# A decoder block on one core: the moving operand of every fp32r matmul is read from its last column to its first, and the accumulator is written in the same order

## The chip, the cores and the metric

The kernel runs on one core of a Trainium2 chip. The metric is the device time of one execution in microseconds (us); smaller is better. The profile calls the engines PE (TensorE, the matrix engine), PEld (its weight loads), DVE (VectorE), ACT (ScalarE), POOL (GpSimd) and SP (SyncE, whose queue carries most DMA transfers). SBUF is the on-chip memory from which PE reads, PSUM the one into which it writes and accumulates.

## What is computed

One decoder block for 256 tokens of width 2048, in float32. Cut to its matrix products:

```python
x = x + 0.5 * swiglu(rmsnorm(x, ffn1_norm), ffn1_w_gate, ffn1_w_up, ffn1_w_down)
proj = rmsnorm(x, mix_norm) @ w_in                      # 2048 x 11264
dq, dk, dv, hq, hf, hi, hg, gate_a, gate_b = split(proj)
y_a = diff_attention(dq, dk, dv, ...)                   # 8 heads
y_b = hgrn2(hq, hf, hi, hg, ...)                        # gated linear recurrence
merged = sigmoid(gate_a) * (y_a @ w_branch_a) + sigmoid(gate_b) * (y_b @ w_branch_b)
x = x + merged @ w_out
x = x + 0.5 * swiglu(rmsnorm(x, ffn2_norm), ffn2_w_gate, ffn2_w_up, ffn2_w_down)
ple = rmsnorm(p @ w_ple_proj, ple_post_norm)
x = x + sigmoid(rmsnorm(x, ple_gate_norm) @ w_ple_gate) * ple
```

The feed-forward width is 5632. In the changed kernel every output has the same value at the same place as before.

## The kernel before

**The products.** All the large products go through one function, `group` (lines 141 to 150). The weights come in blocks of 256 rows by 512 columns, stored as a tile of 128 partitions x 2 x 512. There are 804 such blocks, in the order of the list `plan` (lines 73 to 95): the gate and up matrices of the first feed-forward net, its down matrix, the input projection, the two branch matrices, the output matrix, the second feed-forward net, and the two matrices of the embedding.

**fp32r and three terms.** A float32 operand is split in two fp32r tiles: a high part and the rest. `wh` and `wl` are the two parts of a weight block; `AH` and `AL` (or `hH`/`hL`, `mH`/`mL`, `yaH`/`yaL`, `ybH`/`ybL`, `pH`/`pL`) those of the activations. A product is the sum of three matmuls: high by high (line 148), high by low weights (line 149), low by high weights (line 150).

**Which operand moves.** The stationary operand, loaded into PE's array ahead of each matmul, is a 128 x 128 piece of the activations (128 rows of the sum by 128 tokens). The moving operand, which streams through the array, is half a weight block: 128 partitions by 512 columns, one column after the other. The output is an accumulator `acc` in PSUM of 128 tokens by 512 columns, float32. A block serves two halves of its rows (`k2`) and two token tiles (`tt`), so `group` issues 2 x 2 x 3 = 12 matmuls. In the last product alone, the second token tile is computed as two column halves, in tiles `ms` of 256 columns (`last_product`).

**Order of the work.** The order on every engine is written out by hand. `stream` walks through the blocks of a product: it calls `prep` for the block three places ahead (a DMA on SP's queue into `raw`, line 112; a copy on ACT that makes `wh`, line 114; a subtraction on DVE that makes `wl`, line 115), issues the 12 matmuls, and then lets the smaller tasks go on by a step. These tasks hold the rest of the block: transposes on PE through PSUM tiles `tp` (lines 209, 219, 362), attention (lines 440 to 478), the recurrence (lines 589 to 641), norms and gates on ACT and DVE. Four buffers `acc` take turns, two to a product, so a product writes into the buffers of the product before the last one. `raw` has five buffers, `wh` and `wl` four.

The functions that the change touches, and what calls them:

Of the kernel before, what the change touches and what calls it, by code (L numbers as in the profile page):

```python
# [48 lines left out]
def block_kernel(ctx: ExitStack, tc: tile.TileContext, a: dict, out: bass.AP):  # L49
    nc = tc.nc  # L50
# [15 lines left out]
    def tcol(tt):  # L66
        return slice(tt * P, (tt + 1) * P)
# [73 lines left out]
    def group(n, act, last, dsts):  # L141
        AH, AL = act
        wh, wl = ready[n]
        for k2 in range(2):
            kt = 2 * plan[n][2] + k2
            for dst, tt, cols in dsts:
                hi, lo = AH[:, kt, tcol(tt)], AL[:, kt, tcol(tt)]
                nc.tensor.matmul(dst, hi, wh[:, k2, cols], start=(kt == 0), stop=False)  # L148
                nc.tensor.matmul(dst, hi, wl[:, k2, cols], start=False, stop=False)  # L149
                nc.tensor.matmul(dst, lo, wh[:, k2, cols], start=False, stop=(kt == last))  # L150

    def stream(w, c, groups, act, dsts, held=0):
        for g in range(groups - held):
            n = at[0]
            assert plan[n] == (w, c, g), (plan[n], w, c, g)
            if owed[0]:
                advance()
            prep(n + AHEAD)
            group(n, act, 2 * groups - 1, dsts)
            at[0] += 1  # L160
            owed[0] = True
            if g < groups - 1:
                advance()
# [6 lines left out]
    def last_product(w, c, groups, act):  # L170
        dsts = [(T(psA, [P, NB], "acc"), 0, WHOLE)]
        for cols in (slice(0, HALF), slice(HALF, NB)):
            dsts.append((T(psM, [P, NB], "ms")[:, :HALF], 1, cols))
        stream(w, c, groups, act, dsts, AHEAD)
        for d in dsts:
            for i in range(AHEAD):
                group(at[0] + i, act, 2 * groups - 1, [d])
            yield d
# [717 lines left out]
```

## Time and profile before

| | |
|---|---|
| time before, median of 3 runs | 2307.64 us (2307.3 to 2307.93) |
| the profiled execution's own time | 2307.12 us |
| its span, first to last instruction | 2304.2 us |
| granted TensorE clock, mean | 1.000 |
| PE busy | 2296.5 us, 10564 instructions |
| DVE busy | 1270.9 us, 1381 instructions |
| ACT busy | 1041.0 us, 1270 instructions |
| moved by DMA | 432.55 MB, mean 188 GB/s |

The busy time of an engine is the time in which at least one of its instructions is open. On PE a matmul's record goes on while the next one has begun, so the records of PE sum to more than its busy time; the distance from one start to the next is what a matmul costs in a dense stream. The median of the three runs is 0.52 us above the profiled execution, which is 2.92 us above its own span. A line of the profile names the line of the program, the engine, the operation, output and inputs, the shape, and how often it ran (x).

### The profile page before, as it was taken

How to read it: one execution, taken by the hardware profiler on the slowest of the kernel's cores; microseconds unless marked ns; L12 is line 12 of the kernel's file. 1: busy time of each engine (PE TensorE's matmuls, PEld its weight loads, DVE VectorE, ACT ScalarE, POOL GpSimd, SP SyncE). 2: the span in 40 equal slices, each digit the busy share in tenths (PEclk: the TensorE clock that was granted, in tenths of full speed). 3: DMA queues.
4: the chain of work that ended last, by engine and by line, in shares of the span. 5: the costliest groups of instructions: out<-in, count | busy, mean ns of one | idle time of the engine just before them, and what ended most of it. 6: DMA issues, size and time to landing. Idle time of an engine off the chain costs nothing.

```text
span 2304.2 us, 27206 instructions
## 1 busy us (share of the span) xinstructions
PE 2296.5 (100%) x10564; PEld 1903.1 (83%) x10564; DVE 1270.9 (55%) x1381; ACT 1041.0 (45%) x1270; POOL 39.4 (2%) x38
## 2 busy tenths in 40 slices
PE   9999999999999999999999999999999999999999
PEld 7888888888888888888888888888888888888887
DVE  5555555544444576667765555545555555444456
ACT  6444444444444455553334444544444444344454
POOL 0000000000000100000000000000000000000000
PEclk9999999999999999999999999999999999999999
DMA  8666666666666655554555666666666656666664
GB/s 295 192 190 192 187 189 191 185 192 190 190 186 196 204 159 168 186 173 154 160 159 181 186 189 184 184 192 191 191 186 190 192 186 191 192 190 191 192 211 150
DMA packets 120464, 432.55 MB, mean 188 GB/s; under 512 B 13773, under 2 KB 14181, under 8 KB 120208
## 3 DMA queue, kind: packets, MB, share of 16 engines
q1 hardware_dynamic: 118800, 426.33, 59.7%
q0 software_dynamic: 1248, 4.43, 0.5%
q8 instruction: 82, 1.34, 0.2%
q14 instruction: 46, 0.38, 0.0%
q10 hardware_dynamic: 288, 0.07, 0.0%
HBM read 428.67 MB, written 2.11 MB: 187 GB/s over the span
## 4 chain that ended last, share of the span: by engine, by line
PE 98%; DMA 1%; DVE 0%; ACT 0%; SPq 0%; issue 0%; ACTq 0%
PE acc L148 31%; PE acc L150 31%; PE acc L149 31%; PE tp L209 1%; PE ms L616 1%; DMA raw<-in_gu 1%; PE tp L219 0%; PE ms L440 0%; PE ms L149 0%; PE ms L150 0%; PE ms L148 0%; PE ms L589 0%; PE tp L362 0%; ACT wh L114 0%; PE tp L477 0%
## 5 line engine op out<-in xcount | busy, mean ns | idle before, releaser
L115 DVE TENSOR_TENSOR wl<-raw,wh 128x1024 fp32r<-128x1024 f32 (+1 forms) x805 | 984.1, 1224 | 877.8 <-ACT wh L114 875.6
L114 ACT CAST wh<-raw 128x1024 fp32r<-128x1024 f32 (+1 forms) x805 | 843.8, 1049 | 932.3 <-PE acc L150 904.6
L148 PE MATMUL acc<-wh,AH 128*128 128x512 f32 x2224 | 878.8, 395 | 0.7 <-ACT wh L114 0.5
L150 PE MATMUL acc<-wh,AL 128*128 128x512 f32 x2224 | 868.4, 390 | 0.0
L149 PE MATMUL acc<-wl,AH 128*128 128x512 f32 x2224 | 866.9, 390 | 1.2 <-DVE wl L115 1.0
L150 PEld LDWEIGHTS acc<-wh,AL 128*128 128x128 f32 x2224 | 417.6, 188 | 88.5
L149 PEld LDWEIGHTS acc<-wl,AH 128*128 128x128 f32 x2224 | 418.4, 188 | 85.9 <-DVE wl L115 2.8
L148 PEld LDWEIGHTS acc<-wh,AH 128*128 128x128 f32 x2224 | 418.0, 188 | 85.1 <-ACT wh L114 1.6
L148 PE MATMUL acc<-wh,hH 128*128 128x512 f32 x704 | 275.6, 392 | 0.0
L150 PE MATMUL acc<-wh,hL 128*128 128x512 f32 x704 | 274.5, 390 | 0.0
L149 PE MATMUL acc<-wl,hH 128*128 128x512 f32 x704 | 274.2, 390 | 0.0
L149 PEld LDWEIGHTS acc<-wl,hH 128*128 128x128 f32 x704 | 132.3, 188 | 27.3
L150 PEld LDWEIGHTS acc<-wh,hL 128*128 128x128 f32 x704 | 132.2, 188 | 27.4
L148 PEld LDWEIGHTS acc<-wh,hH 128*128 128x128 f32 x704 | 132.2, 188 | 27.0
L263 ACT ACTIVATE s<-acc,rowr 128x256 f32<-128x256 f32 x86 | 40.6, 475 | 48.9 <-PE acc L150 48.9
L183 ACT CAST hH<-tp 128x512 fp32r<-128x512 f32 x44 | 25.8, 587 | 73.9 <-PE tp L209 73.9
L184 DVE TENSOR_TENSOR hL<-tp,hH 128x512 fp32r<-128x512 f32 x44 | 30.4, 692 | 45.9 <-ACT hH L183 45.8
L265 DVE SCALAR_TENSOR_TENSOR h<-acc,rowr,s 128x256 f32<-128x256 f32 x86 | 41.5, 484 | 19.4 <-ACT s L263 19.4
L148 PE MATMUL acc<-wh,mH 128*128 128x512 f32 x128 | 50.7, 396 | 0.0
L150 PE MATMUL acc<-wh,mL 128*128 128x512 f32 x128 | 50.0, 391 | 0.0
L149 PE MATMUL acc<-wl,mH 128*128 128x512 f32 x128 | 49.9, 390 | 0.0
L186 ACT ACTIVATE AH<-tp,gains 128x256 fp32r<-128x256 f32 x48 | 22.8, 475 | 30.5 <-PE tp L209 16.5
(191 smaller groups left out, 1018.2 us busy)
## 6 DMA issues: line engine op xcount, KB each, us to landing
raw<-in_gu SPq DMA_DIRECT2D x351, 512.0 KB, 3.6
raw<-in_down SPq DMA_DIRECT2D x176, 512.0 KB, 3.9
raw<-in_w_in SPq DMA_DIRECT2D x176, 512.0 KB, 3.6
raw<-in_w_out SPq DMA_DIRECT2D x32, 512.0 KB, 3.9
raw<-in_w_pg SPq DMA_DIRECT2D x32, 512.0 KB, 4.1
raw<-in_w_a SPq DMA_DIRECT2D x16, 512.0 KB, 3.5
raw<-in_w_b SPq DMA_DIRECT2D x16, 512.0 KB, 3.6
junk<-in_xT SPq DMA_DIRECT2D x8, 256.0 KB, 3.5
```

Of the source, the lines that this page charges most:

```text
L114: nc.scalar.copy(wh[:, ks, :], raw[:, ks, :])
L115: nc.vector.tensor_tensor(wl[:, ks, :], raw[:, ks, :], wh[:, ks, :].bitcast(F32), op=ALU.subtract)
L148: nc.tensor.matmul(dst, hi, wh[:, k2, cols], start=(kt == 0), stop=False)
L149: nc.tensor.matmul(dst, hi, wl[:, k2, cols], start=False, stop=False)
L150: nc.tensor.matmul(dst, lo, wh[:, k2, cols], start=False, stop=(kt == last))
L183: nc.scalar.copy(H, src)
L184: nc.vector.tensor_tensor(L, src, H.bitcast(F32), op=ALU.subtract)
L186: nc.scalar.activation(H, src, AF.Copy, scale=gain)
L209: nc.tensor.transpose(tp[:, i, tcol(tt)], src_of(tt, kt + i), ident)
L263: nc.scalar.activation(s, acc[tt][:, :HALF], AF.Silu, scale=rs[0][:, tt : tt + 1])
L265: nc.vector.scalar_tensor_tensor(h[tt], acc[tt][:, HALF:], rs[0][:, tt : tt + 1], s, op0=ALU.mult, op1=ALU.mult)
L616: nc.tensor.matmul(lp[:, i, tt, :], km[:, i, tt, :], q4[:, i, tt, :], start=True, stop=True)
```

## The change

In `group`, the output and the moving operands are turned round: the views `dst`, `wh[:, k2, cols]` and `wl[:, k2, cols]` start at their last column and go back by one element a step. The stationary operands are as before. Column j of the weights still goes to column j of the accumulator; it is the order in time that is turned, column 511 first and column 0 last (255 to 0 in the tiles `ms`). All 9696 matmuls of lines 148 to 150 are changed, no other matmul, and nothing on ACT, DVE, POOL or the DMA queues is written differently. The instruction as built carries the new walk: its output and its moving operand begin 511 elements into the row, with a step of -1.

```diff
             kt = 2 * plan[n][2] + k2
             for dst, tt, cols in dsts:
                 hi, lo = AH[:, kt, tcol(tt)], AL[:, kt, tcol(tt)]
-                nc.tensor.matmul(dst, hi, wh[:, k2, cols], start=(kt == 0), stop=False)
-                nc.tensor.matmul(dst, hi, wl[:, k2, cols], start=False, stop=False)
-                nc.tensor.matmul(dst, lo, wh[:, k2, cols], start=False, stop=(kt == last))
+                back = dst[:, ::-1]
+                whr, wlr = wh[:, k2, cols][:, ::-1], wl[:, k2, cols][:, ::-1]
+                nc.tensor.matmul(back, hi, whr, start=(kt == 0), stop=False)
+                nc.tensor.matmul(back, hi, wlr, start=False, stop=False)
+                nc.tensor.matmul(back, lo, whr, start=False, stop=(kt == last))
```

Lines 148 to 150 become lines 150 to 152, and all lines behind them move on by two. The instructions on each engine stand in the same order as before. What differs besides the walk is a few waits that the framework sets: PE carries waits on its own counter (`PE_49`) at 105 rows before and at 121 now, 27 added and 11 dropped, and seven rows of line 115 on DVE no longer wait for PE (they still wait for the DMA and for ACT). Two places on PE show both kinds. The first is the start of the third product of the first feed-forward net; before:

```order
L148 MATMUL acc_508<-wh_437,AH_97 128x512 [waits Activation_49]
L149 MATMUL acc_508<-wl_438,AH_97 128x512 [waits DVE_49]
L150 MATMUL acc_508<-wh_437,AL_98 128x512
L148 MATMUL acc_509<-wh_437,AH_97 128x512
L149 MATMUL acc_509<-wl_438,AH_97 128x512
L150 MATMUL acc_509<-wh_437,AL_98 128x512
```

The same rows of the changed kernel:

```order
L150 MATMUL acc_508<-wh_437,AH_97 128x512 [waits Activation_49]
L151 MATMUL acc_508<-wl_438,AH_97 128x512 [waits DVE_49]
L152 MATMUL acc_508<-wh_437,AL_98 128x512
L150 MATMUL acc_509<-wh_437,AH_97 128x512 [waits PE_49]
L151 MATMUL acc_509<-wl_438,AH_97 128x512
L152 MATMUL acc_509<-wh_437,AL_98 128x512
```

The first matmul into the product's second accumulator now waits on PE's own counter. The following product starts in this way in the kernel before already:

```order
L148 MATMUL acc_684<-wh_623,AH_97 128x512 [waits Activation_49]
L149 MATMUL acc_684<-wl_624,AH_97 128x512 [waits DVE_49]
L150 MATMUL acc_684<-wh_623,AL_98 128x512
L148 MATMUL acc_685<-wh_623,AH_97 128x512 [waits PE_49]
L149 MATMUL acc_685<-wl_624,AH_97 128x512
L150 MATMUL acc_685<-wh_623,AL_98 128x512
```

The other place is in the input projection, where four transposes of a tile `tok` stand between two blocks; before:

```order
L150 MATMUL acc_7656<-wh_7596,AL_3744 128x512
L219 MATMUL tp_7675<-ident_94,tok_7649 128x128 [waits DVE_49,PE_49]
L219 MATMUL tp_7675<-ident_94,tok_7649 128x128 x3
L148 MATMUL acc_7655<-wh_7614,AH_3743 128x512 [waits Activation_49]
L149 MATMUL acc_7655<-wl_7615,AH_3743 128x512
```

And now:

```order
L152 MATMUL acc_7656<-wh_7596,AL_3744 128x512
L221 MATMUL tp_7675<-ident_94,tok_7649 128x128 [waits DVE_49]
L221 MATMUL tp_7675<-ident_94,tok_7649 128x128 x3
L150 MATMUL acc_7655<-wh_7614,AH_3743 128x512 [waits Activation_49]
L151 MATMUL acc_7655<-wl_7615,AH_3743 128x512
```

Here a wait on PE's own counter is gone from the first transpose.

## The prediction

> **What bounds the kernel now.** I read the profile's first part and its chain of waits first, then the waits of PE alone, then the dense stream itself in the timeline.
>
> ```profile
> PE 2296.5 (100%) x10564; PEld 1903.1 (83%) x10564; DVE 1270.9 (55%) x1381; ACT 1041.0 (45%) x1270; POOL 39.4 (2%) x38
> PE 98%; DMA 1%; DVE 0%; ACT 0%; SPq 0%; issue 0%; ACTq 0%
> PE acc L148 31%; PE acc L150 31%; PE acc L149 31%; PE tp L209 1%; PE ms L616 1%; DMA raw<-in_gu 1%; PE tp L219 0%; PE ms L440 0%; PE ms L149 0%; PE ms L150 0%; PE ms L148 0%; PE ms L589 0%; PE tp L362 0%; ACT wh L114 0%; PE tp L477 0%
> ```
>
> PE is at work for 2296.5 us of a span of 2304.2, and the chain that ends last is PE for 98%, nearly all of it in the three lines that the change rewrites. The waits of PE (engine, line, waited for: us in total, times, longest) say the same from the other side:
>
> ```profile
> PE ms L290 <- DVE warm L287: 1.2, 1, 1.2
> PE acc L149 <- DVE wl L115: 1.0, 2, 0.8
> PE acc L148 <- ACT wh L114: 0.5, 1, 0.5
> ```
>
> PE's idle time that these rows put on other engines is 2.7 us in all. So the kernel is as fast as PE takes its instructions, and a change of the moving stream goes into the time one for one. How many matmuls there are is shown by the windows view over the whole span for lines 148, 149 and 150, one after the other, and by the groups of the narrow tiles:
>
> ```profile
> 0.00:2304.20 2304.20, 1270.61 (x3232) 607.35 (x3232) 1.00 0.61 188
> ...
> 0.00:2304.20 2304.20, 1256.14 (x3232) 607.86 (x3232) 1.00 0.61 188
> ...
> 0.00:2304.20 2304.20, 1258.14 (x3232) 606.94 (x3232) 1.00 0.61 188
> ...
> L148 PE MATMUL ms<-wh,AH 128*128 128x256 f32 x32 | 9.0, 281 | 0.0
> ```
>
> That is 3 x 3232 = 9696 matmuls. Each line has 32 with 256 columns, so 9600 have 512 columns and 96 have 256. The granted clock (1.00) stands in the same rows. What one costs is the distance between starts, not its record (0.39 us here); a stretch without any other instruction, 33 distances from the first row to the last:
>
> ```profile
> 1000.08 0.39 PE L148 MATMUL acc<-wh,AH 128*128 128x512 f32 x1
> 1000.31 0.39 PE L149 MATMUL acc<-wl,AH 128*128 128x512 f32 x1
> 1000.53 0.39 PE L150 MATMUL acc<-wh,AL 128*128 128x512 f32 x1
> ...
> 1007.56 0.39 PE L148 MATMUL acc<-wh,AH 128*128 128x512 f32 x1
> ```
>
> (1007.56 - 1000.08) / 33 = 226.7 ns for 512 columns. The last product ends with a run of narrow ones, 35 distances:
>
> ```profile
> 2295.12 0.28 PE L148 MATMUL ms<-wh,AH 128*128 128x256 f32 x1
> 2295.23 0.28 PE L149 MATMUL ms<-wl,AH 128*128 128x256 f32 x1
> ...
> 2299.31 0.28 PE L150 MATMUL ms<-wh,AL 128*128 128x256 f32 x1
> ```
>
> (2299.31 - 2295.12) / 35 = 119.7 ns for 256 columns. The two give a price per column, (226.7 - 119.7) / 256 = 0.418 ns, and a fixed part per matmul, 226.7 - 512 x 0.418 = 12.7 ns. The whole: 9600 x 226.7 ns + 96 x 119.7 ns = 2176.3 + 11.5 = 2187.8 us, 95% of the span. The other 116.4 us are the 10564 - 9696 = 868 matmuls of other lines, and the two ends; the change leaves them alone.
>
> **The change, part by part.** Instructions: none is added, removed or moved. The stationary operands, the bytes read and written, and the order of the matmuls are as they were, so three things are left to be priced.
>
> First, the column price. No row of this kernel shows a matmul with a step other than one, so it has to be bounded. From below: nothing, since the same 512 elements are read in the same number of 4-byte steps, and a column can't be dropped; I see no way in which the price per column falls. From above, the nearest rows are those of an engine that takes one element after the other from the same kind of data, ACT's copy of `raw` in two lengths:
>
> ```profile
> L114 ACT CAST wh<-raw 128x1024 fp32r<-128x1024 f32 x803 | 842.5, 1050 | 931.2 <-PE acc L150 904.6 <-issue 8.3 <-PE ms L150 6.5
> L114 ACT CAST wh<-raw 128x512 fp32r<-128x512 f32 x2 | 1.2, 612 | 1.1 <-DMA raw<-in_gu 1.1
> ```
>
> (1050 - 612) / 512 = 0.855 ns per element, 2.05 times PE's 0.418. PE takes float32 columns at twice the rate of an engine that reads the same memory. If it does so by fetching two neighbours at once, the question is whether the pairs still form on the way down. They are the same pairs: going up, elements 0 and 1, 2 and 3, up to 510 and 511; going down from 511, elements 511 and 510 and so on to 1 and 0. A row of 512 or 256 elements has no odd one left over. A unit that pairs by address finds each pair in the same eight bytes; only one that asks for a step of exactly +1 loses them. The same holds for the writes to PSUM, which go down over the same pairs. I take the price as unchanged, and keep the twofold price as a rival.
>
> Second, the fixed part of 12.7 ns. It could grow if the start at the far end of a row costs something at the beginning of each matmul, and shrink if it holds something that depends on the direction. A matmul and the next one walk in the same direction in both kernels, and where they share an accumulator the new one begins at the column that the old one wrote longest ago. What a hand-over has to respect is the same, and I take no change. As bounds I use once the fixed part more, and the whole of it less: 9696 x 12.7 ns = 123.1 us either way.
>
> Third, the waits. 27 matmuls get a wait on PE's own counter, 11 lose one, and seven subtractions on DVE lose a wait for PE. What such a wait costs is to be seen at the start of the fourth product, where the kernel before already has one, at the matmul that starts at 75.44:
>
> ```profile
> 75.22 0.39 PE L150 MATMUL acc<-wh,AL 128*128 128x512 f32 x1
> 75.44 0.39 PE L148 MATMUL acc<-wh,AH 128*128 128x512 f32 x1
> 75.67 0.39 PE L149 MATMUL acc<-wl,AH 128*128 128x512 f32 x1
> ```
>
> It starts 0.22 us after the one ahead and its successor 0.23 us later: nothing is lost, since what it waits for, an earlier matmul into the same buffer, ended a whole product ago. Queued behind it are only PE's own matmuls; nobody else is held. If each of the 27 cost as much as the dearest regular break in the stream, the first matmul behind a set of transposes, it would be this:
>
> ```profile
> 54.77 0.60 PE L209 MATMUL tp<-ident,h 128*128 128x128 f32 x4
> 55.12 0.48 PE L148 MATMUL acc<-wh,AH 128*128 128x512 f32 x1
> 55.44 0.39 PE L149 MATMUL acc<-wl,AH 128*128 128x512 f32 x1
> ```
>
> 0.32 us in place of 0.227, so 0.09 us each and 27 x 0.09 = 2.4 us in all, 0.1%. I take nothing. The seven waits that DVE loses can't bring anything, as DVE is busy for 55% of the span and PE waited for its `wl` for only 1.0 us.
>
> The sum: 9600 x 0 + 96 x 0 + 27 x 0 = 0. Against the profiled execution this leaves a span of 2304.2 us and a time of 2307.1; the median of the runs is 0.5 us above that, so I name 2307.6 us.
>
> **The rivals.** *Half the rate (slower).* The place is each of the 9696 matmuls; the mechanism is that columns come, or results go, singly when the step is -1. A column then costs 2 x 0.418 ns, so a wide matmul takes 214.0 ns more and a narrow one 107.0: 9600 x 214.0 + 96 x 107.0 ns = 2054.4 + 10.3 = 2064.7 us, and the time is 4372 us. At ACT's own rate it would be 4469 (0.4375 ns more per column: 2150 + 11 us). It decides from the first fraction, as nothing on the path covers PE: 0.5 ns per matmul is 4.8 us, the 0.2% that a measurement of this kernel can tell from no change. For it speaks that PE's rate is so close to twice that of a single-element reader; against it that every pair stays whole. [...] I give this rival 0.15, all larger losses included.
>
> *A dearer start (slower).* The fixed part grows, because the first fetch now opens a row at its end. Between 0.5 ns a matmul (4.8 us) and once the 12.7 ns (123.1 us), so between 2312 and 2431 us. For it: a part of 12.7 ns exists, and the trace doesn't show of what it is made. Against it: the weight load for the next matmul and all addresses are known well ahead in such a stream. 0.14.
>
> *A cheaper start (faster).* If the 12.7 ns hold a conflict between the end of one stream and the start of the next that depends on the direction, up to 123.1 us come back: 2307.6 - 123.1 = 2184.5 us at most. Since two neighbouring matmuls walk in the same direction in both kernels, I see no reason for it: 0.05.
>
> *The walk isn't turned at all.* Were the two reversals cancelled when the program is made, the stream would be the old one, at 2307.6 us. The instruction as built does carry the last element as its start and -1 as its step, so this can only be in the hardware's hands; its time is that of my forecast and it is held within that chance.
>
> **How the numbers follow.** No change of over 0.2%: 0.66. Slower: 0.14 + 0.15 = 0.29. Faster: 0.05. The likeliest case gives 2307.6 us, with a range of its own of 2303 to 2312. Left out of the range are half the rate (0.15) and the cheaper start (0.05), 2 in 10 together; it takes in the dearer start up to its bound. So it runs from 2303 to 2307.6 + 123.1 = 2431 us.
>
> **What would show it.** Right: the dense stretch of the first feed-forward net has 226.7 ns from start to start, narrow matmuls 119.7, PE's own waits stay at 2.7 us or so, and the matmuls with an added wait start 0.23 us behind the one ahead. Half the rate: about 440 ns and 227 ns, with ACT and DVE idle for longer in their waits for `acc` and the same busy time. A dearer start: the same number of ns added to wide and narrow matmuls alike. A cost of the waits: 27 single breaks at the start of a product, and a stream that is unchanged between them. The forecast is wrong if the distance between starts differs from 226.7 by over 0.5 ns.

## The result and the profile after

The changed kernel takes 2364.65 us (median of 3 runs, 2364.24 to 2365.85) against 2307.64 us: 1.0248 times as long, 95% interval [1.0225, 1.0272]. The forecast of no change was wrong. The profiled execution took 2364.24 us, with a span of 2362.1, which is 57.9 us more than before, at the same clock of 1.000.

The page's busy times and its chain have the form that they had, with PE still on the path throughout:

```profile
PE 2355.0 (100%) x10564; PEld 1905.2 (81%) x10564; DVE 1272.5 (54%) x1381; ACT 1036.9 (44%) x1270; POOL 39.5 (2%) x38
PE 99%; DMA 0%; DVE 0%; SPq 0%; ACT 0%; issue 0%
```

DVE and ACT have nearly the same busy time as before (1270.9 and 1041.0 us there); PE alone has 58.5 us more. A settled stretch of the changed kernel (timeline; start us, length us, engine, line), 36 distances from the first row to the last:

```profile
708.42 0.40 PE L151 MATMUL acc<-wl,hH 128*128 128x512 f32 x1
...
716.82 0.40 PE L151 MATMUL acc<-wl,hH 128*128 128x512 f32 x1
```

(716.82 - 708.42) / 36 = 233.3 ns from start to start, in place of 226.7. The narrow matmuls of the last product, 33 distances:

```profile
2353.09 0.28 PE L150 MATMUL ms<-wh,AH 128*128 128x256 f32 x1
...
2357.00 0.28 PE L150 MATMUL ms<-wh,AH 128*128 128x256 f32 x1
```

That is 118.5 ns, no more than the 119.7 of before. PE's waits for other engines are 2.3 us in all (2.7 before):

```profile
PE ms L292 <- DVE warm L289: 1.2, 1, 1.2
PE acc L151 <- DVE wl L115: 0.8, 1, 0.8
PE acc L150 <- ACT wh L114: 0.3, 1, 0.3
```

And the place of the first added wait, the matmul nine places ahead of the first transposes (which start at 55.90), shows no break either; it starts at 53.80:

```profile
53.57 0.40 PE L152 MATMUL acc<-wh,AL 128*128 128x512 f32 x1
53.80 0.40 PE L150 MATMUL acc<-wh,AH 128*128 128x512 f32 x1
54.04 0.40 PE L151 MATMUL acc<-wl,AH 128*128 128x512 f32 x1
```

So the loss is 6.7 ns in most of the 9600 wide matmuls. The trace has 9445 distances from one wide matmul to the next. Of these, 8414 are below 229 ns before and none after; paired row by row with the changed kernel, they grew by 6.72 ns on average, 56.6 us in all. Another 877 lie between 229 and 245 ns before already, 841 of them among the first 14 behind a set of transposes or other small matmuls; these grew by only 0.86 ns on average, 0.8 us in all. The two groups hold 57.3 of the 57.9 us.

### The profile page after: what moved, and what is told of

Its sections match the earlier page's. It is cut to its first block, busy times and chain, and to the rows that moved or that the text cites. A ratio compares the mean times of both kernels' runs of the same rounds, so it can differ in the third digit from the quotient of the medians.

```text
span 2362.1 us, 27200 instructions
## 1 busy us (share of the span) xinstructions
PE 2355.0 (100%) x10564; PEld 1905.2 (81%) x10564; DVE 1272.5 (54%) x1381; ACT 1036.9 (44%) x1270; POOL 39.5 (2%) x38
## 4 chain that ended last, share of the span: by engine, by line
PE 99%; DMA 0%; DVE 0%; SPq 0%; ACT 0%; issue 0%
PE acc L150 32%; PE acc L151 32%; PE acc L152 32%; PE tp L211 1%; PE ms L618 1%; PE tp L221 0%; DMA raw<-in_gu 0%; PE ms L442 0%; PE ms L152 0%; PE ms L151 0%; PE ms L150 0%; PE ms L591 0%; PE tp L364 0%; PE ms L643 0%; PE tp L480 0%; PE tp L479 0%
## 5 line engine op out<-in xcount | busy, mean ns | idle before, releaser
L150 PE MATMUL acc<-wh,AH 128*128 128x512 f32 x2224 | 894.1, 402 | 0.4 <-ACT wh L114 0.3
L151 PE MATMUL acc<-wl,AH 128*128 128x512 f32 x2224 | 884.3, 398 | 0.8 <-DVE wl L115 0.8
L152 PE MATMUL acc<-wh,AL 128*128 128x512 f32 x2224 | 884.0, 397 | 0.0
L150 PE MATMUL acc<-wh,hH 128*128 128x512 f32 x704 | 280.9, 399 | 0.0
L152 PE MATMUL acc<-wh,hL 128*128 128x512 f32 x704 | 279.8, 397 | 0.0
L151 PE MATMUL acc<-wl,hH 128*128 128x512 f32 x704 | 279.8, 397 | 0.0
```

The lines of the kernel that those rows point to most:

```text
L150: nc.tensor.matmul(back, hi, whr, start=(kt == 0), stop=False)
L151: nc.tensor.matmul(back, hi, wlr, start=False, stop=False)
L152: nc.tensor.matmul(back, lo, whr, start=False, stop=(kt == last))
```

## The experiments

All of them edit `group` of the kernel before. What is measured is the distance from start to start in settled stretches, beside the kernel's time. A stretch is settled where the distances have become steady or repeat in a fixed pattern; of a pattern the mean is given.

**The reading side alone.**

```diff
+                whr, wlr = wh[:, k2, cols][:, ::-1], wl[:, k2, cols][:, ::-1]
+                nc.tensor.matmul(dst, hi, whr, start=(kt == 0), stop=False)
+                nc.tensor.matmul(dst, hi, wlr, start=False, stop=False)
+                nc.tensor.matmul(dst, lo, whr, start=False, stop=(kt == last))
```

> Only the moving operand is read from its last column to its first; the accumulator is written upwards as before, so the columns of every large product land mirrored. In the changed kernel a 512-column matmul takes 233.3 ns from start to start in place of 226.7. If the 6.7 ns belong to the reading side (theory 1), they are all here: 233.3 ns and 2364 us. If they belong to the writing side (theory 2), this is 226.7 ns and 2307.6 us. If they come only when both are turned, also 226.7 ns here and in the kernel that turns the writes alone.

**The writing side alone.**

```diff
+                back = dst[:, ::-1]
+                nc.tensor.matmul(back, hi, wh[:, k2, cols], start=(kt == 0), stop=False)
+                nc.tensor.matmul(back, hi, wl[:, k2, cols], start=False, stop=False)
+                nc.tensor.matmul(back, lo, wh[:, k2, cols], start=False, stop=(kt == last))
```

> Only the accumulator is written from its last column to its first; the moving operand is read upwards as before (columns land mirrored). Theory 1 (the reading side pays): 226.7 ns from start to start, 2307.6 us. Theory 2 (the writing side pays): 233.3 ns, 2364 us.

With the reads turned the kernel took 2365.1 us, 1.0249 times the kernel before [1.0232, 1.0266]; with the writes turned 2307.54 us, 0.9998 [0.9989, 1.0008]. Two rows of the first kernel's timeline, 36 distances apart:

```profile
153.80 0.40 PE L150 MATMUL acc<-wl,AH 128*128 128x512 f32 x1
...
162.20 0.40 PE L150 MATMUL acc<-wl,AH 128*128 128x512 f32 x1
```

And the same of the second:

```profile
153.82 0.39 PE L151 MATMUL acc<-wh,AL 128*128 128x512 f32 x1
...
161.98 0.39 PE L151 MATMUL acc<-wh,AL 128*128 128x512 f32 x1
```

233.3 and 226.7 ns. The reading side pays everything, the writing side nothing. The second kernel writes with a step of -1 into PSUM in every product and, as built, carries the same 27 added waits as the changed kernel; the first carries none of them. So neither the writes nor the waits are left as a cause.

**Is it one price per matmul, or one per column?** First two kernels in which the three matmuls of a term have 512, 448 and 384 columns, upwards and downwards.

```diff
+                full = cols.stop - cols.start
+                n1, n2 = (448, 384) if full == NB else (full, full)
...
+                nc.tensor.matmul(dst[:, :n1], hi, wlv[:, :n1], start=False, stop=False)
+                nc.tensor.matmul(dst[:, :n2], lo, whv[:, :n2], start=False, stop=(kt == last))
```

> The kernel before (upwards), with the second matmul of each three cut to the first 448 columns and the third to 384; left out are the other columns of these two terms. It is the base for the next kernel. From a column price of 0.417 ns and a fixed part of 13.3 ns: 226.7, 200.0 and 173.3 ns from the start of the 512-, 448- and 384-column matmul to the next start, and about 2307.6 - 3200 x (26.7 + 53.3) ns = 2052 us if PE still bounds the kernel.

> The same three widths, read and written downwards (first columns 511, 447 and 383). If a turned matmul costs a fixed 6.7 ns more (theory A, a dearer start): 233.3, 206.7 and 180.0 ns, 64 us more than the kernel with these widths upwards. If the columns are dearer by 6.7 / 512 = 0.013 ns each (theory B): 233.3, 205.8 and 178.3 ns, 56 us more. If the narrow matmuls of the last product were unchanged because only the columns beyond 256 are dearer (theory C, 0.026 ns each): 233.3, 205.0 and 176.7 ns, 48 us more.

They took 2090.24 and 2103.26 us, a difference of 13 us where 48 to 64 were expected, and the base was 38 us slower than worked out. With mixed widths the upward stream did not settle at all: its distances behind a 512-column matmul were spread from 230 to 241 ns, where the downward stream stood at 233.3. So the pair decided nothing. It showed that 226.7 ns is not a property of an upward matmul as such, but something that an even stream settles into.

**Orders of the walk.** In the next kernel each pair of products of the two feed-forward nets has an even stream of its own, and only the reads are turned.

```diff
+    SET = [(0, 1), (0, -1), (-256, 1), (256, -1), (-16, 1), (16, -1), (-4, 1), (4, -1), (-2, 1), (2, -1), (0, 1)]
+    def walk(dst, t, block, step):
...
+        t = t.rearrange("p (b m) -> p b m", m=m)
+        t = t[:, ::-1, :] if block < 0 else t
+        t = t[:, :, ::-1] if step < 0 else t
```

> The kernel before, with the read order of the 512 columns changed in the gate and up products of both feed-forward nets, two products to an order (192 matmuls without the first of each sum): up; down; two blocks of 256, the upper first, up inside; two blocks in order, down inside; the same pair of orders for blocks of 16, 4 and 2; up again. The accumulator is written upwards, so columns land in other places. Start to start is 226.7 ns upwards and 233.3 downwards. Theory A (a fixed price, once per matmul, for a downward innermost step): 233.3 for all orders that go down inside, 226.7 for those that go up inside. Theory B (each run of falling addresses pays a little): the price grows with the number of falls, so blocks of 256 the upper first is 226.7, and blocks of 2 are dearest. Theory C (the place of the first element in its 16 bytes): 233.3 where the first element is the last of its 16 bytes (down; down inside blocks of 256, 16 and 4), 226.7 for the orders that go up inside blocks of 4 and more.

A second kernel of this kind was made when these results were known; it has the other sizes of a block, and orders that turn the 16-byte lines but not the elements in them. A 16-byte line means four neighbouring fp32r columns, counted from the start of the row.

```diff
+        if inner:
+            t = t.rearrange("p (b i k) -> p b i k", i=m // k, k=k)[:, :, ::-1, :]
```

> As the kernel of the walks, with other read orders of the 512 columns, written upwards. First net: up, down, then blocks of 8, 32, 64 and 128 columns, each once with the blocks from last to first and up inside, and once with the blocks in order and down inside. Second net: blocks of 8, 16, 32, 64, 128 and 256 in order, inside a block the 16-byte lines from last to first, inside a line upwards; blocks of 8, 16 and 4 in order with the pairs inside from last to first; down; up. The kernel of the walks gave 226.7 ns where only the order inside a 16-byte line was turned (blocks of 4 and 2), 233.3 where the lines fall throughout, 266.7 for blocks of 16 down inside. If nothing but the order of the 16-byte lines counts (theory L): each order with lines from last to first equals the one with the same blocks and down inside, blocks of 16 give 266.7 again, blocks of 4 with turned pairs 226.7. If the direction of the innermost step counts as well (theory A), those that go up inside a line stay at 226.7. Blocks from last to first with up inside: 233.3 ns by theory L while a block is shorter than some hundred bytes and 226.7 for blocks of 128, as for 256.

The two together, in ns from start to start for 512 columns; both nets gave the same where an order ran in both:

| block, columns (bytes) | blocks from last to first, up inside | blocks in order, down inside | blocks in order, 16-byte lines from last to first inside, up in a line |
|---|---|---|---|
| 2 (8) | 233.3 | 226.7 | |
| 4 (16) | 233.3 | 226.7 | |
| 8 (32) | 233.3 | 233.3 | 233.3 |
| 16 (64) | 233.3 | 266.7 | 266.7 |
| 32 (128) | 232.5 | 233.3 | 233.3 |
| 64 (256) | 226.7 | 233.3 | 233.3 |
| 128 (512) | 226.7 | 233.3 | 233.3 |
| 256 (1024) | 226.7 | 233.3 | 233.3 |

Rows of the first kernel: up; all down; blocks of 16 down inside; blocks of 4 down inside. Each pair is 36 distances apart.

```profile
36.00 0.39 PE L167 MATMUL acc<-wh,AH 128*128 128x512 f32 x1
...
44.16 0.39 PE L167 MATMUL acc<-wh,AH 128*128 128x512 f32 x1
...
84.66 0.40 PE L168 MATMUL acc<-wl,AH 128*128 128x512 f32 x1
...
93.06 0.40 PE L168 MATMUL acc<-wl,AH 128*128 128x512 f32 x1
...
270.31 0.43 PE L168 MATMUL acc<-wl,AH 128*128 128x512 f32 x1
...
279.92 0.43 PE L168 MATMUL acc<-wl,AH 128*128 128x512 f32 x1
...
363.13 0.39 PE L168 MATMUL acc<-wl,AH 128*128 128x512 f32 x1
...
371.29 0.39 PE L168 MATMUL acc<-wl,AH 128*128 128x512 f32 x1
```

226.7, 233.3, 266.7 and 226.7 ns. And two pairs of the second kernel: blocks of 16 with the lines turned but every line read upwards, and blocks of 4 with the two pairs in them turned:

```profile
1558.35 0.43 PE L175 MATMUL acc<-wl,AH 128*128 128x512 f32 x1
...
1567.95 0.43 PE L175 MATMUL acc<-wl,AH 128*128 128x512 f32 x1
...
1885.83 0.39 PE L175 MATMUL acc<-wl,AH 128*128 128x512 f32 x1
...
1893.99 0.39 PE L175 MATMUL acc<-wl,AH 128*128 128x512 f32 x1
```

266.7 and 226.7 ns. This settles what is counted. The last two columns of the table are equal row by row (233.3, 266.7 and 233.3 ns for blocks of 8, 16 and 32, and so on): in the orders that were tried it doesn't matter how the four elements of a 16-byte line are read, only in which order the lines come. A step of -1 inside a line is free, 226.7 ns for blocks of 4 (theory A falls). A row whose lines fall throughout pays 6.7 ns in all (233.3), and eight blocks of 64 that each fall pay no more than the one row does (233.3; theory B falls). Rises of 256 bytes or more are enough to be free (226.7 from blocks of 64 on, 232.5 for blocks of 32), though the blocks themselves fall. Blocks of 64 bytes in order, with their four lines falling, are by far the dearest (266.7), for which no theory here had a reason.

**The first column, and the width once more.** The same kind of kernel, with another first column or another width in each pair of products.

```diff
+    def walk(dst, t, width, first, step):
+        return dst[:, :width], t[:, first : first + width][:, ::step]
```

> The kernel before, with the moving operand's first column and width changed in the gate and up products, two products to a case; the columns beyond the width are left out of all but the first term of each sum. First net, 480 columns: upwards from column 0, 1, 2, 3, 4 and 16, downwards to column 0, 1, 2, 3 and 16. Second net: 512, 448, 384, 320 and 288 columns, each upwards and downwards. Upwards from column 0 I expect 0.4167 ns per column and 13.3 ns more: 213.3, 200.0, 173.3, 146.7 and 133.3 ns for 480, 448, 384, 320 and 288. Theory A (fixed price of a downward step): every downward case 6.7 ns above the upward one of its width, whatever the first column. Theory C (the place of the first element): upward from 1, 2 and 3 dearer than from 0, 4 and 16, and the downward cases differ among themselves by their first column. Theory D (a price per column): 6.3, 5.8, 5.0, 4.2 and 3.8 ns for 480, 448, 384, 320 and 288 columns downwards.

> The widths again, more finely: gate and up products with 512, 496, 464, 448, 432, then 416, 400, 384, 352, 336 columns, each upwards and downwards; the other columns are left out of all but the first term. The first kernel of widths had +6.7 ns downwards for 512, +4.5 for 384, 0 for 320, with 448 unsteady from product to product. A price per column from a threshold on (theory T): it grows evenly from 0 at 320 to 6.7 at 512, so +1.1 at 352, +3.3 at 416, +5.6 at 480. A fixed price that the weight load hides in short matmuls: 6.7 ns down to some width, then nothing. Neither: no order in the differences, since the upward stream itself settles at different distances by width.

For 480 columns upwards from column 0, 1, 2, 3, 4 and 16 the distances were 216.7, 220.0, 213.3, 216.7, 216.7 and 218.3 ns; downwards to 0, 1, 2, 3 and 16 they were 220.0, 222.2, 222.2, 220.0 in one product and 226.7 in the other, and 218.3. So the place of the first column does matter, in both directions, and theory C's order (0, 4 and 16 cheap) isn't found: upwards from column 2 is cheapest, at 213.3 ns. Over both kernels, by width; "beside the columns" is what is left after 0.4167 ns per column, which is (226.7 - 146.7) / 192 from 512 and 320 columns upwards:

| columns | up, ns | down, ns | beside the columns, up | and down | difference |
|---|---|---|---|---|---|
| 512 | 226.7 | 233.3 | 13.3 | 20.0 | 6.7 |
| 496 | 223.3 | 226.7 | 16.7 | 20.0 | 3.3 |
| 448 | 206.7 | 206.7 | 20.0 | 20.0 | 0.0 |
| 416 | 188.4 | 191.1 | 15.0 | 17.8 | 2.7 |
| 400 | 180.0 | 182.2 | 13.3 | 15.6 | 2.2 |
| 384 | 173.3 | 177.8 | 13.3 | 17.8 | 4.5 |
| 352 | 160.0 | 162.2 | 13.3 | 15.6 | 2.2 |
| 336 | 153.3 | 153.3 | 13.3 | 13.3 | 0.0 |
| 320 | 146.7 | 146.7 | 13.3 | 13.3 | 0.0 |
| 288 | 131.7 | 133.3 | 11.7 | 13.3 | 1.6 |

448 upwards stood at 202.6 in one product of the first kernel; 464 and 432 differed between products by 1.0 and 0.3 ns upwards. Two pairs of rows from the first kernel, 384 columns up and down, 36 distances each:

```profile
1646.60 0.33 PE L165 MATMUL acc<-wh,AH 128*128 128x384 f32 x1
...
1652.84 0.33 PE L165 MATMUL acc<-wh,AH 128*128 128x384 f32 x1
...
1681.51 0.34 PE L165 MATMUL acc<-wh,AH 128*128 128x384 f32 x1
...
1687.91 0.34 PE L165 MATMUL acc<-wh,AH 128*128 128x384 f32 x1
```

Neither a fixed price nor one per column comes out, so theories A, D and T fall as laws of the width. From 320 columns on and with column 0 at one end, the part beside the columns lies between 13.3 and 20.0 ns in either direction, and where it settles depends on the width and the direction; with another first column it went up to 26.7 ns (480 columns down to column 3). The 512-column stream of the kernel before is at the low end of that (13.3), and turned it is at the high end (20.0).

**The weight load beside it.** The stationary operand and mixed directions.

```diff
+        "gu1": [("uuu",), ("ddd",), ("uuu", 2), ("ddd", 2), ("uuu", 4), ("ddd", 4), ("uuu", 16), ("ddd", 16),
+                ("udu",), ("dud",), ("uud",)],
+        "gu2": [("uuu", "m64"), ("ddd", "m64"), ("uuu", "m32"), ("ddd", "m32"), ("uuu", "hi"), ("ddd", "hi"),
+                ("uuu", "wh"), ("ddd", "wh"), ("uuu", 8), ("ddd", 8), ("ddd",)],
```

> All moving operands are 512 columns, written upwards. What varies, two products of the gate and up matrices to a case, is the stationary operand and the direction of the three matmuls of a term: all up or all down with the stationary piece as it is; with the piece of the first token tile shifted by 2, 4, 16 or 8 tokens (other tokens are multiplied there); with 64 or 32 of its 128 columns loaded (the other tokens are left out of the sums); with the high part in place of the low part of the activations; with the high part of the weights in place of the low part; and three mixed directions (up down up, down up down, up up down). [...] Theory Q (falling 16-byte lines cost a fixed 6.7 ns at the start of the moving stream itself): 226.7 ns up and 233.3 ns down in every case, and in the mixed cases 6.7 ns for each matmul that goes down, so 228.9, 231.1 and 228.9 ns on average.

Downwards the distance was 233.3 to 233.4 ns in all nine cases: any shift, 128, 64 or 32 loaded columns, any pair of operands. Upwards it was not constant: 226.7 with the pieces as they are, with the high part twice, and with one weight tile thrice; 230.5, 231.1 and 232.2 with a shift of 2, 8 and 16; with a shift of 4 it was 226.7 in one product and 232.2 in the next; 230.0 and 231.7 with 64 and 32 loaded columns. Rows upwards with 64 loaded columns, then downwards, 36 distances each:

```profile
1507.21 0.40 PE L169 MATMUL acc<-wl,AH 128*64 128x512 f32 x1
...
1515.49 0.40 PE L169 MATMUL acc<-wl,AH 128*64 128x512 f32 x1
...
1552.67 0.40 PE L169 MATMUL acc<-wl,AH 128*64 128x512 f32 x1
...
1561.08 0.40 PE L169 MATMUL acc<-wl,AH 128*64 128x512 f32 x1
```

Up down up gave 227, 233 and 227 ns, 228.9 on average, one price for one turned matmul as theory Q has it; but down up down gave 240, 230 and 230, 233.3 on average, and up up down 231.1. A change of the weight load moves the difference between the directions, from 6.7 ns down to 1.1 (a shift of 16) or 3.3 (64 loaded columns), but it is the upward stream that loses its 226.7 ns, while the downward one stays at 233.3 to 233.4. Theory Q is right on the downward stream alone. What sets the upward stream's rhythm stays open.

**The whole kernel in other orders.** Reads and writes alike, so that all columns land where they belong.

```diff
+    def turn(t):
+        return t.rearrange("p (b m) -> p b m", m=4)[:, :, ::-1]
...
+        return t.rearrange("p (b m) -> p b m", m=64)[:, ::-1, :]
...
+        return t.rearrange("p (b m) -> p b m", m=16)[:, :, ::-1]
```

> The whole kernel with every row walked in order of its blocks of 4 columns, 16 bytes, and downwards inside each block, reads and writes alike. Every element is still read and written with a step of -1 inside its block. If only the order of the 16-byte lines counts (theory L): 226.7 ns from start to start and 2307.6 us. If the step of -1 itself cost the 6.7 ns (theory A): 233.3 ns and 2364 us.

> The whole kernel with the blocks of 64 columns taken from last to first, upwards inside a block, reads and writes alike. The first column is 448 and the last one 63. Theory L with runs of 256 bytes upwards: 226.7 ns and 2307.6 us. If it were the direction over the whole row, or that the row is begun in its last part and ended in its first: 233.3 ns and 2364 us.

> The whole kernel with the blocks of 16 columns in order and downwards inside a block, reads and writes alike. The kernel of the walks had 266.7 ns there, so 9600 x 40.0 ns = 384 us more than before, about 2692 us with the narrow matmuls unchanged. If the 40 ns were a matter of that kernel's mix of products: 233.3 ns as in the changed kernel, 2364 us.

Turned inside the 16-byte lines: 2307.28 us, 1.0000 times the kernel before [0.999, 1.001]. Blocks of 64 columns from last to first: 2307.35 us, 0.9998 [0.9989, 1.0007]. Blocks of 16 down inside: 2683.51 us, 1.163 [1.1607, 1.1653]. The distances are 226.7, 226.7 and, from the third kernel's rows, 266.7 ns:

```profile
702.91 0.43 PE L154 MATMUL acc<-wh,hL 128*128 128x512 f32 x1
...
712.51 0.43 PE L154 MATMUL acc<-wh,hL 128*128 128x512 f32 x1
```

What the walks showed in parts of the kernel holds for its whole time, up to a price six times that of the change. The third kernel is 8 us below the expected 2692, which fits the matmuls that stood above 226.7 ns before: the 877 of them named above grew by 34.0 ns on average, the 8414 settled ones by 40.0.

**Two bytes an element.**

```diff
+                    mv, d = walk(wl[:, k2, cols], *WALKS[plan[n][1] // 2]), dst
+                    for _ in range(3):
+                        nc.tensor.matmul(d, warm[:, :P], mv, start=False, stop=False)
```

> The second gate and up products with all but the first and last two of each sum's 16 row blocks in bf16: moving operand bf16 (2 bytes an element), stationary operand a tile of zeros, so these terms are left out of the sums. Read orders, two products each: up; down; blocks of 256 and of 64 from last to first, up inside; blocks of 256 and 64 in order, down inside; blocks of 16 from last to first, up inside; blocks of 16, 32 and 8 in order, down inside; down. If the price belongs to the order of 16-byte lines whatever the element (theory L): down dearer than up, blocks of 8 in order and down inside (one line of 16 bytes) as cheap as up, and blocks of 32 (64 bytes) the dearest. If it is a matter of four-byte elements alone, that is of the rate at which lines are used up: the same time for all orders.

Every order took 215.8 ns, blocks of 32 down inside as well. A row of the downward products (77 matmuls merged in 16.78 us; without the last one's 0.38 us that is 76 distances of 215.8 ns):

```profile
1535.49 16.78 PE L164 MATMUL acc<-wl,warm 128*128 128x512 bf16 x77
```

So theory L, as worded there, falls for bf16. Two things differ from fp32r: 512 bf16 columns lie on 64 lines of 16 bytes (215.8 ns), 512 fp32r columns on 128 (226.7), and the stationary operand is bf16 too. The last kernel keeps the second and undoes the first: its bf16 columns are every second one, over the same lines as fp32r columns.

```diff
+                    top = wh.rearrange("p k n -> p (k n)").bitcast(BF16).rearrange("p (k n u) -> p k n u", k=2, u=2)[:, k2, :, 1]
+                    mv, d = walk(top, *WALKS[plan[n][1] // 2]), dst
```

> As the bf16 kernel, but the moving operand is the upper two bytes of each fp32r element of the high part of the weights, every second bf16 element, so that 512 columns pass over the same 128 lines of 16 bytes as fp32r columns do, at two bytes used of four; the stationary operand is a bf16 tile of zeros again (these terms are left out). Same read orders: up; down; blocks of 256 and 64 from last to first; blocks of 256 and 64 in order, down inside; blocks of 16 from last to first; blocks of 16, 32 and 8 in order, down inside; down. The plain bf16 stream took 215.8 ns in every order. Theory L1 (what counts is the rate at which 16-byte lines are used up, one in 1.7 ns for fp32r, half that for bf16): the price comes back, dearer down than up, dearest for blocks of 16 down inside. Theory L2 (it is a matter of fp32r matmuls, with their four-byte stationary operand): 215.8 ns in every order.

The price is back: 225.0 ns up, 231.1 down; 225.0 for blocks of 256 and 64 from last to first, 231.1 for the same blocks in order and down inside; 233.3 for blocks of 16 from last to first, and 266.7 for blocks of 16 down inside; 231.1 for blocks of 32. Blocks of 8 down inside are at 225.3, where fp32r had 233.3. Merged rows of blocks of 256 from last to first, blocks of 256 in order and down inside, and blocks of 16 down inside:

```profile
1561.64 17.72 PE L160 MATMUL acc<-wh,warm 128*128 128x512 bf16 x78
...
1605.87 18.19 PE L160 MATMUL acc<-wh,warm 128*128 128x512 bf16 x78
...
1786.81 20.43 PE L160 MATMUL acc<-wh,warm 128*128 128x512 bf16 x76
```

Without the last record (0.38 to 0.43 us) these are 77, 77 and 75 distances of 225.2, 231.3 and 266.7 ns. L2 falls, and L1 holds but for the blocks of 8: neither fp32r nor the four-byte weight load is needed for the price, which is 6.1 ns here (231.1 - 225.0). What this stream and the fp32r stream have in common, and the dense bf16 stream has not, is four bytes from one column to the next, one 16-byte line in 1.7 ns (4 x 0.4167). The upward stream too is 9.2 ns dearer over these lines than the dense bf16 stream (225.0 - 215.8). This suggests, and does not show, that most of the 13.3 ns beside the columns in the kernel before has the same origin.

## Why the prediction was wrong

- **That PE is the whole bound, and a change of its stream goes into the time one for one:** right. Of the 57.9 us by which the span grew, 56.6 are 6.7 ns in each of the 8414 matmuls that were settled.
- **The waits cost nothing:** right; the place of the first added wait shows no break (0.23 us behind the one ahead, its successor 0.24 us later), PE's waits for others did not grow (2.3 us, 2.7 before), and the kernel that turns the writes has the same 27 waits at 2307.54 us.
- **The column price, "the price as unchanged":** right in the sense meant there. Half the rate did not come (2364.65 us, not 4372), and PSUM written downwards costs nothing (0.9998 of the time before). But the argument, pairs of eight bytes that stay whole, looked at the wrong unit: inside 16 bytes every order that was tried is free (226.7 ns), and the order of the 16-byte lines is what is paid for (233.3). That ACT takes single elements and PE two at once was my reading of their prices, 0.855 and 0.418 ns an element; no run shows it. I had no row of a falling line and did not name that case.
- **The fixed part, "What a hand-over has to respect is the same, and I take no change":** this is the step that failed. The 12.7 ns (13.3 in a settled stream) became 20.0. The argument spoke only of the accumulator, on the writing side, which the runs show to be free (2307.54 us); it left out the reading side, which alone pays the whole price (2365.1 us) through the order in which the 16-byte lines come.
- **The rival of a dearer start** gave 2312 to 2431 us and holds the measured time, with about half of its bound (6.7 of 12.7 ns). Its sign that wide and narrow matmuls grow alike was wrong: 256 columns did not grow (118.5 against 119.7), and by width the difference jumps between 0 and 6.7 ns. Its mechanism, a first fetch at the far end of a row, is not it either: blocks of 64 columns from last to first begin at column 448 and cost nothing (2307.35 us). That the range held the measured time is thus luck as far as the mechanism goes; what was shown is a price that is there once per matmul at 512 columns.

What stays open is why an upward stream of 512 columns settles at the low end and a downward one at the high end, why blocks of 64 bytes with falling lines cost 40 ns more (266.7 against 226.7), and what sets the upward rhythm when the weight load changes. All orders tried inside one instruction were regular ones; a row that falls only at its start or only at its end was not tried.

## What to carry to other kernels

In a kernel like this one, with TensorE as the bound and four bytes from one column of the moving operand to the next, rising addresses are the order to take first: 226.7 ns a matmul of 512 columns against 233.3 downwards. If columns have to come in another order, three ways were free here: blocks of 256 bytes or more from last to first (226.7 ns, the whole kernel 0.9998), turning inside 16 bytes (226.7 ns, 1.0000), or turning the writes into PSUM instead (0.9998). What rising addresses bring depends on the width and on the stationary piece: at 320, 336 and 448 columns the two directions cost the same (146.7, 153.3 and 206.7 ns), and with a shifted piece the upward stream was only 1.1 to 2.9 ns cheaper in all products but one. An engine's distance from start to start, split into a price per column and a rest, says where a new pattern may hit: a rest that isn't understood is to be priced, not taken as constant (12.7 ns here, which became 20.0). The dense bf16 stream, with two bytes a column, stood at 215.8 ns in every order tried.

## What the runs showed of the hardware that was not expected

- The order of reading inside a 16-byte line was free (226.7 ns with blocks of 4 columns read down), that of the lines was not: 226.7 ns up, 233.3 down, 266.7 when the four lines of each 64 bytes fall, for 512 fp32r columns.
- Writing the accumulator with a step of -1 cost nothing: 0.9998 of the time before [0.9989, 1.0008].
- The dense fp32r stream is slower than the dense bf16 stream by 10.9 ns a matmul (226.7 against 215.8), and a bf16 stream over the same lines by 9.2 (225.0).
- Even the order before is not always at 226.7 ns: a shift of the stationary piece by 16 tokens, or fewer loaded columns, put the same upward stream at 230.0 to 232.2 ns.
